# When a chunk's rows are normalised, and how the last two rows of the output are weighted, in a hybrid encoder block on one Trainium2 core

## The chip, the core and the metric

One core of a Trainium2 chip runs the whole program. Its engines work side by side, each from an instruction queue of its own: TensorE (PE, with its weight loads as PEld) multiplies matrices, VectorE (DVE), ScalarE (ACT) and GpSimd (POOL) do elementwise work, SyncE (SP) issues most of the DMA transfers; ACT issues some too. Engines wait for each other by semaphores. The metric is the device time of one execution in microseconds.

## The reference

One encoder layer over 1024 tokens of width 1024, all in float32: a combined projection, windowed attention and a bidirectional gated-DeltaNet mixer on its parts, an output projection with a residual, and a feed-forward part with squared ReLU. What matters here is the second half:

```python
def _rmsnorm(x, w):
    x32 = x.astype(jnp.float32)
    y = x32 * lax.rsqrt(jnp.mean(x32 * x32, axis=-1, keepdims=True) + EPS)
    return (y * w.astype(jnp.float32)).astype(x.dtype)
...
        h = h + jnp.concatenate([attn, gdn], axis=-1) @ w_out[l]
        hn = _rmsnorm(h, norm_ffn_w[l])
        h = h + jnp.square(jax.nn.relu(hn @ w_ffn_in[l])) @ w_ffn_out[l]
    return _rmsnorm(h, norm_final_w)
```

## The kernel before

The 1024 tokens are eight chunks of 128 rows. `h[c]` is the tile of chunk c, 128 x 1024, with tokens on the partitions. Every float32 product is made of three matmuls (`mm3`, lines 124 to 126) over a high and a low part of each operand; `split` makes the parts: ACT copies the high part (L119), POOL subtracts it (L120).

The program is written as Python generators that are woven together; a scheduler then places the instructions in one fixed queue per engine, with an eye on priorities and on free buffers of the pools. The queues are what the order listings below show.

Around the change in the middle of the program run three generators. `scan(1, ...)` goes backwards over the chunks (7 down to 0) and finishes the mixer's rows `o` of a chunk; its small products are L797. `out_all` takes the chunks in the same order. For each it prepares the mixer's part (`out_gdn`): four Squares on ACT with their sums (L900), four small steps on DVE (L902 to L905), a power on POOL (L906), a scaling on DVE (L907), four transposes on PE (L910), a multiply out of PSUM on DVE (L911), and the split. Then `out_gemm` multiplies with the output weights: two halves of twelve matmuls, each added to `h[c]` by DVE (L876). At L926 SP stores the sum to memory. Up to three chunks are prepared ahead: in the text of the program the preparation of chunk c - 3 stands right behind the sum of chunk c and ahead of the product of chunk c - 1.

The finished rows are normalised by `norm_h`, which calls `norm_rows`: a Square over the whole row on ACT with its sum (L203), two POOL steps for the reciprocal root (`rstd`, L190 and L191), and a scaling on DVE (L205). For chunks 7 to 4 the scaling writes in place, over the tile that L926 stores; for 3 to 0 it writes another tile. Before, chunks 7 to 4 are normalised together when all four are summed, at the head of `tokens_second` (`norm_half(1)`), and each of 3 to 0 when it is summed, if four rows are there already. `tokens_second` transposes the four rows on PE (L209) into feed-forward operands (L966, L214, L215, L970, L949, L950). It is woven with the rest of `out_all`.

At the end of the program `second_products` makes the last product group P4, row by row, for rows 4 to 7; each row's sum is finished by DVE (L1199), and `finish` normalises it: Square on ACT (L1229), `rstd` on POOL, one DVE instruction that scales and weights (L1232), and a store from SP (L1233). The last row, 7, is finished by `finish_last` in two halves of 512 columns, the upper of which is complete earlier; its halves are scaled by ACT (L1220) and DVE (L1221) and stored from ACT and SP (L1223).

Of the kernel before, what the change touches and what calls it, by code (L numbers as in the profile page):

```python
# [11 lines left out]
BF16 = mybir.dt.bfloat16  # L12
AF = mybir.ActivationFunctionType
ALU = mybir.AluOpType
AX = mybir.AxisListType

P = 128
SEQ = 1024
D = 1024
NT = SEQ // P  # L20
NK = D // P
HALF = 512
GH = 4
DFF = 4096
EPS = 1e-6
# [52 lines left out]
class Block:  # L78
# [837 lines left out]
    def out_all(self, chunks):  # L916
# [3 lines left out]
        for n, c in enumerate(chunks):  # L920
# [6 lines left out]
            self.summed.append(c)  # L927
            if c < 4 and len(self.rows) >= 4:
                self.norm_h(c)

# [247 lines left out]
    def second_products(self, n, p, left, right, banks, last):  # L1178

        nc = self.nc  # L1180
        bank, tag = {"P1": ("a", "psA"), "P2": ("b", "psB"), "P5": ("c", "psB"), "P7": ("d", "psA"), "P6": ("a", None),
                     "P3": ("c", None), "P4": ("d", None)}[p]
        lo, hi = slice(0, HALF), slice(HALF, D)
        for i in range(4):
            ps = banks[bank, i] = self.ps(tag) if tag else banks[bank, i]
# [10 lines left out]
            if p == "P4" and last and i == 3:  # L1196
                self.finish_last(7, ps)
                continue
# [4 lines left out]
            if last and p in ("P3", "P4"):  # L1203
                self.finish(i if p == "P3" else 4 + i)

    def finish_last(self, t, ps):

        nc = self.nc
        lo, hi = slice(0, HALF), slice(HALF, D)
        h = self.h[t]  # L1210
        ss, rs = self.small((P, 2)), self.small((P, 1))
        scr, hw, o = self.pt((P, HALF), BF16), [self.pt(), self.pt()], [self.pt(), self.pt()]
        nc.scalar.activation(out=scr, in_=h[:, hi], func=AF.Square, accum_out=ss[:, 1:2])
        nc.gpsimd.tensor_tensor(out=hw[1], in0=h[:, hi], in1=self.w_fin[:, hi], op=ALU.mult)
        nc.vector.tensor_tensor(out=h[:, lo], in0=h[:, lo], in1=ps, op=ALU.add)
        nc.scalar.activation(out=scr, in_=h[:, lo], func=AF.Square, accum_out=ss[:, 0:1])
        nc.vector.tensor_tensor(out=hw[0], in0=h[:, lo], in1=self.w_fin[:, lo], op=ALU.mult)
        nc.vector.tensor_tensor(out=ss[:, 0:1], in0=ss[:, 0:1], in1=ss[:, 1:2], op=ALU.add)
        self.rstd(ss[:, 0:1], rs)
        nc.scalar.activation(out=o[0], in_=hw[0], func=AF.Copy, scale=rs)  # L1220
        nc.vector.tensor_scalar(out=o[1], in0=hw[1], scalar1=rs, scalar2=None, op0=ALU.mult)  # L1221
        for i, sl in enumerate((lo, hi)):
            (nc.scalar, nc.sync)[i].dma_start(out=self.io["out"][0, t * P:(t + 1) * P, sl], in_=o[i])  # L1223

    def finish(self, t):
# [152 lines left out]
```

## Time and profile before

| | |
|---|---|
| runs | 1255.85, 1256.17, 1258.47 us; median 1256.17 |
| the profiled execution | 1255.02 us, of which the span of the trace is 1253.3 |
| mean granted clock of TensorE | 0.983 of full speed |
| matmuls and transposes on PE | 6482 |

A row of the timeline reads: start in us, duration in us, engine, line, operation, output tile <- inputs, shapes, count; in brackets the idle time of the engine ahead of it and what ended that. On PE the printed duration is longer than the distance to the next matmul, since matmuls are pipelined; distances are taken from the starts. Rows of stages give, for each stretch, the busy time of PE, PEld, DVE, ACT and POOL with the number of instructions, the granted clock of TensorE as a share, the DMA engines' busy share and GB/s.

### The profile page before, as it was taken

Reading aid. Unit: us, or ns where it says so; the run is one execution under the profiler, and the core shown is the slowest. Engines: PE = TensorE matmul, PEld = TensorE weight load, DVE = VectorE, ACT = ScalarE, POOL = GpSimd, SP = SyncE. Lnnn points to the kernel's source line nnn. Section 1 sums busy time; section 2 is a strip of 40 time slices with the busy share of each in tenths; the row PEclk is TensorE's granted clock in tenths of the full one; section 3 lists DMA queues with packets and bytes.
Section 4 is the critical chain, followed back from the end, with each engine's and each line's share of the span. In section 5 each row is a group of like instructions: output and inputs, shape, how many; then the busy total and the mean of one; then the engine's idle time right before and its main releaser. Section 6 shows DMA issues by size and latency. Waiting matters only on the chain.

```text
span 1253.3 us, 18527 instructions
## 1 busy us (share of the span) xinstructions
PE 1191.6 (95%) x6482; PEld 967.2 (77%) x6482; DVE 854.9 (68%) x1528; ACT 621.4 (50%) x1347; POOL 580.3 (46%) x488
## 2 busy tenths in 40 slices
PE   7999999899789989998999999999999999999997
PEld 5778777677568868877788888888777888888885
DVE  5667667982389986676655454544668797886976
ACT  6455688335485752125464554545545434444343
POOL 5354211362432433144573534535445665655595
PEclk9999999899889999998999999999999999999999
DMA  7134344441956678122234344443678624434323
GB/s 239 52 121 133 101 171 140 139 126 40 223 168 158 190 216 296 60 84 85 84 131 159 132 151 143 154 159 134 223 280 280 223 85 167 151 121 148 95 90 135
DMA packets 121630, 187.62 MB, mean 150 GB/s; under 512 B 11043, under 2 KB 64416, under 8 KB 121537
## 3 DMA queue, kind: packets, MB, share of 16 engines
q1 hardware_dynamic: 96708, 152.58, 37.9%
q10 hardware_dynamic: 16381, 29.67, 6.3%
q0 software_dynamic: 8448, 4.20, 1.9%
q8 instruction: 51, 0.84, 0.3%
q14 instruction: 42, 0.34, 0.1%
HBM read 122.39 MB, written 63.49 MB: 148 GB/s over the span
## 4 chain that ended last, share of the span: by engine, by line
PE 49%; DVE 6%; DMA 3%; issue 2%; POOL 1%; ACT 1%; ACTq 0%; POOLq 0%; DVEq 0%; SPq 0%
PE psA L124 8%; PE psA L125 8%; PE psA L126 8%; PE psB L126 7%; PE psB L125 7%; PE psB L124 7%; DMA pg<-sd 3%; PE psB L797 2%; DVE pg L1154 1%; DVE pt L1163 1%; DVE wr L1166 1%; PE psB L209 1%; DVE pg L1199 1%; DMA sd<-pt 0%; DVE wr L1161 0%
## 5 line engine op out<-in xcount | busy, mean ns | idle before, releaser
L124 PE MATMUL psA<-pg,wh 128*128 128x512 f32 x416 | 167.6, 404 | 2.1 <-ACT pt L458 2.1
L126 PE MATMUL psA<-pg,wl 128*128 128x512 f32 x416 | 166.9, 401 | 0.0
L125 PE MATMUL psA<-pg,wh 128*128 128x512 f32 x416 | 166.5, 400 | 0.0
L120 POOL TENSOR_TENSOR wl<-wr,wh 128x512 fp32r<-128x512 f32 x44 | 70.2, 1618 | 154.0 <-ACT wh L119 153.9
L1154 DVE TENSOR_TENSOR pg<-pg 128x512 fp32r<-128x512 f32 x112 | 122.7, 1127 | 18.8 <-ACT pg L1153 18.6
L120 POOL TENSOR_TENSOR wh<-wr,wh 128x512 fp32r<-128x512 f32 x32 | 47.9, 1518 | 131.5 <-ACT wh L119 131.5
L1071 ACT ACTIVATE pt<-pt 128x512 f32<-128x512 f32 x64 | 40.4, 632 | 122.7 <-DVE pt L1061 122.7
L125 PE MATMUL psA<-pg,pg 128*128 128x512 f32 x256 | 99.7, 391 | 0.5 <-POOL pg L120 0.5
L124 PE MATMUL psA<-pg,pg 128*128 128x512 f32 x256 | 99.0, 391 | 1.0 <-DVE pg L1199 1.0
L126 PE MATMUL psA<-pg,pg 128*128 128x512 f32 x256 | 99.7, 389 | 0.0
L120 POOL TENSOR_TENSOR pg<-wr,pg 128x512 fp32r<-128x512 f32 x48 | 73.4, 1560 | 51.0 <-ACT pg L119 51.0
L124 PEld LDWEIGHTS psA<-pg,wh 128*128 128x128 f32 x416 | 79.2, 190 | 21.3 <-ACT pt L458 2.4
L125 PEld LDWEIGHTS psA<-pg,wh 128*128 128x128 f32 x416 | 79.3, 191 | 19.7 <-issue 0.9
L126 PEld LDWEIGHTS psA<-pg,wl 128*128 128x128 f32 x416 | 79.1, 190 | 18.6
L1153 ACT CAST pg<-pg 128x512 fp32r<-128x512 f32 x112 | 67.2, 620 | 41.3 <-DMA pg<-sd 31.0
L126 PE MATMUL psB<-pg,pg 128*128 128x512 f32 x192 | 75.0, 390 | 1.3 <-DVE pg L1154 1.3
L125 PE MATMUL psB<-pg,pg 128*128 128x512 f32 x192 | 75.0, 391 | 0.8 <-POOL pg L120 0.7
L124 PE MATMUL psB<-pg,pg 128*128 128x512 f32 x192 | 74.7, 390 | 0.4 <-ACT pg L1153 0.4
L119 ACT CAST wh<-wr 128x512 fp32r<-128x512 f32 x76 | 43.6, 623 | 45.5 <-PE psA L125 24.8
L1061 DVE TENSOR_TENSOR pt<-psB,pt 128x512 f32<-128x512 f32 x39 | 26.9, 689 | 55.1 <-PE psB L126 30.1
L1061 DVE TENSOR_TENSOR pt<-psA,pt 128x512 f32<-128x512 f32 x39 | 26.8, 689 | 55.0 <-PE psA L126 39.5
L124 PEld LDWEIGHTS psA<-pg,pg 128*128 128x128 f32 x256 | 48.0, 188 | 12.6 <-DVE pg L1199 2.3
(385 smaller groups left out, 3307.7 us busy)
## 6 DMA issues: line engine op xcount, KB each, us to landing
sd<-pt ACTq DMA_DIRECT2D x112, 256.0 KB, 2.2
pg<-sd SPq DMA_DIRECT2D x112, 256.0 KB, 2.9
wr<-in_w_ffn_in SPq DMA_DIRECT2D x32, 512.0 KB, 3.8
wr<-in_w_in SPq DMA_DIRECT2D x22, 512.0 KB, 4.8
pg<-in_x SPq DMA_DIRECT2D x16, 512.0 KB, 5.4
wr<-in_w_ffn_out SPq DMA_DIRECT2D x16, 512.0 KB, 4.8
sc<-kvd SPq DMA_DIRECT2D x14, 512.0 KB, 4.1
kvd<-pt SPq DMA_DIRECT2D x16, 256.0 KB, 2.8
```

Of the source, the lines that this page charges most:

```text
L119: nc.scalar.copy(out=h, in_=raw)
L120: (eng or nc.gpsimd).tensor_tensor(out=l, in0=raw, in1=h.bitcast(F32), op=ALU.subtract)
L124: nc.tensor.matmul(ps, wh, xh, start=first, stop=False, skip_group_check=onto)
L125: nc.tensor.matmul(ps, wh, xl, start=False, stop=False, skip_group_check=onto)
L126: nc.tensor.matmul(ps, wl, xh, start=False, stop=last, skip_group_check=onto)
L209: self.nc.tensor.transpose(ps[:, i * P:(i + 1) * P], row[:, k * P:(k + 1) * P], self.ident)
L797: nc.tensor.matmul(ps[:, h - g.start, :], left(h), right[:, h, :], start=True, stop=True)
L1061: self.nc.vector.tensor_tensor(out=out, in0=in0, in1=in1, op=ALU.add)
L1071: self.nc.scalar.activation(out=c, in_=c, func=AF.Relu)
L1153: nc.scalar.copy(out=s[:, 0], in_=raw)
L1154: v.tensor_tensor(out=s[:, 1], in0=raw, in1=s[:, 0].bitcast(F32), op=ALU.subtract)
L1163: v.tensor_tensor(out=b["T2"], in0=b["B22"], in1=b["T1"], op=ALU.subtract)
```

## The change

Two things are changed. In `out_all`, `norm_h(c)` follows every chunk's sum, for all eight chunks; `norm_half` then finds nothing left to do. At the end, row 6 is no longer finished by `finish`: its two halves are multiplied with the weight by DVE (`weighted`, L1215 of the changed kernel), its Square and `rstd` are as before, and one DVE instruction scales it at the end of `finish_last` (L1242). In `finish_last` itself the sum of squares of the upper half is scaled by a POOL step of its own (L1230), a second POOL step joins the halves (L1234) and takes the place of a DVE addition, the multiply of the upper half on POOL is dropped, and DVE scales and weights the upper half in one instruction (L1237).

```diff
--- before.py
+++ after.py
@@ -925,8 +925,7 @@
             yield from self.out_gemm(self.h[c], *ready.pop(0), self.wo[1])
             self.nc.sync.dma_start(out=self.hd[c], in_=self.h[c])
             self.summed.append(c)
-            if c < 4 and len(self.rows) >= 4:
-                self.norm_h(c)
+            self.norm_h(c)
 
 
     def norm_h(self, c):
@@ -1194,33 +1193,54 @@
             dst = {"P1": self.h[i][:, lo], "P2": self.h[i][:, lo], "P6": u2, "P5": self.h[4 + i][:, hi],
                    "P7": self.h[4 + i][:, hi], "P3": self.h[i][:, hi], "P4": self.h[4 + i][:, lo]}[p]
             if p == "P4" and last and i == 3:
-                self.finish_last(7, ps)
+                self.finish_last(7, ps, self.held)
                 continue
             nc.vector.tensor_tensor(out=dst, in0=dst, in1=ps, op=ALU.add)
             if last and p == "P6":
                 for d in (self.h[i][:, hi], self.h[4 + i][:, hi], self.h[4 + i][:, lo]):
                     nc.gpsimd.tensor_tensor(out=d, in0=d, in1=u2, op=ALU.add)
             if last and p in ("P3", "P4"):
-                self.finish(i if p == "P3" else 4 + i)
-
-    def finish_last(self, t, ps):
+                if p == "P4" and i == 2:
+                    self.held = self.weighted(6, hw, 0)
+                else:
+                    self.finish(i if p == "P3" else 4 + i)
+                if p == "P4" and i == 1:
+                    hw = self.wr((P, D))
+                    self.weighted(6, hw, 1)
+
+    def weighted(self, t, hw, part):
+
+        nc = self.nc
+        sl = slice(part * HALF, (part + 1) * HALF)
+        nc.vector.tensor_tensor(out=hw[:, sl], in0=self.h[t][:, sl], in1=self.w_fin[:, sl], op=ALU.mult)
+        if part == 0:
+            ss, rs = self.small((P, 1)), self.small((P, 1))
+            nc.scalar.activation(out=self.pt((P, D), BF16), in_=self.h[t], func=AF.Square, accum_out=ss)
+            self.rstd(ss, rs)
+            return t, hw, rs
+
+    def finish_last(self, t, ps, held):
 
         nc = self.nc
         lo, hi = slice(0, HALF), slice(HALF, D)
         h = self.h[t]
         ss, rs = self.small((P, 2)), self.small((P, 1))
-        scr, hw, o = self.pt((P, HALF), BF16), [self.pt(), self.pt()], [self.pt(), self.pt()]
+        scr, hw, o = self.pt((P, HALF), BF16), self.pt(), [self.pt(), self.pt()]
         nc.scalar.activation(out=scr, in_=h[:, hi], func=AF.Square, accum_out=ss[:, 1:2])
-        nc.gpsimd.tensor_tensor(out=hw[1], in0=h[:, hi], in1=self.w_fin[:, hi], op=ALU.mult)
+        nc.gpsimd.tensor_scalar(out=ss[:, 1:2], in0=ss[:, 1:2], scalar1=1.0 / D, scalar2=EPS, op0=ALU.mult, op1=ALU.add)
         nc.vector.tensor_tensor(out=h[:, lo], in0=h[:, lo], in1=ps, op=ALU.add)
         nc.scalar.activation(out=scr, in_=h[:, lo], func=AF.Square, accum_out=ss[:, 0:1])
-        nc.vector.tensor_tensor(out=hw[0], in0=h[:, lo], in1=self.w_fin[:, lo], op=ALU.mult)
-        nc.vector.tensor_tensor(out=ss[:, 0:1], in0=ss[:, 0:1], in1=ss[:, 1:2], op=ALU.add)
-        self.rstd(ss[:, 0:1], rs)
-        nc.scalar.activation(out=o[0], in_=hw[0], func=AF.Copy, scale=rs)
-        nc.vector.tensor_scalar(out=o[1], in0=hw[1], scalar1=rs, scalar2=None, op0=ALU.mult)
+        nc.vector.tensor_tensor(out=hw, in0=h[:, lo], in1=self.w_fin[:, lo], op=ALU.mult)
+        nc.gpsimd.tensor_scalar(out=ss[:, 0:1], in0=ss[:, 0:1], scalar1=1.0 / D, scalar2=ss[:, 1:2], op0=ALU.mult,
+                                op1=ALU.add)
+        nc.gpsimd.tensor_tensor(out=rs, in0=ss[:, 0:1], in1=self.nhalf_exp[:, :1], op=ALU.pow)
+        nc.vector.scalar_tensor_tensor(out=o[1], in0=h[:, hi], scalar=rs, in1=self.w_fin[:, hi], op0=ALU.mult, op1=ALU.mult)
+        nc.scalar.activation(out=o[0], in_=hw, func=AF.Copy, scale=rs)
         for i, sl in enumerate((lo, hi)):
             (nc.scalar, nc.sync)[i].dma_start(out=self.io["out"][0, t * P:(t + 1) * P, sl], in_=o[i])
+        t, hw, rs = held
+        nc.vector.tensor_scalar(out=hw, in0=hw, scalar1=rs, scalar2=None, op0=ALU.mult)
+        nc.sync.dma_start(out=self.io["out"][0, t * P:(t + 1) * P, :], in_=hw)
 
     def finish(self, t):
         nc = self.nc
```

What the scheduler made of it stands in the queues. First ACT, around the preparations of chunks 4 and 3 (`pg_4322` is `o` of chunks 5 and 4, `pg_4019` of chunks 3 and 2; `pt_5653`, `pt_5679`, `pt_5705` are the split of chunks 7, 6 and 5; `wl` and `wh` rows belong to feed-forward weights). Before:

```order
L119 CAST pt_5576<-wr_5574 128x512
L900 ACTIVATE scr_5743,sm_5741<-pg_4322 128x128 x4
L900 ACTIVATE scr_5798,sm_5796<-pg_4019 128x128 x4
L119 CAST wl_5623<-wr_5612 128x512
L119 CAST wh_5617<-wr_5610 128x512
L119 CAST wh_5620<-wr_5610 128x512
L119 CAST pt_5653<-wr_5631 128x512
L900 ACTIVATE scr_5853,sm_5851<-pg_4019 128x128 x3
L119 CAST pt_5679<-wr_5657 128x512
```

In the changed kernel (`pg_4973`, `pg_5076`, `pg_5165` are `h` of chunks 7, 6 and 5):

```order
L119 CAST pt_5679<-wr_5657 128x512
L119 CAST wl_5628<-wr_5612 128x512
L119 CAST pt_5705<-wr_5683 128x512
L203 ACTIVATE pt_5740,sm_5738<-pg_4973 128x1024
L900 ACTIVATE scr_5750,sm_5748<-pg_4322 128x128 x4
L119 CAST pt_5767<-wr_5745 128x512
L203 ACTIVATE pt_5802,sm_5800<-pg_5076 128x1024
L900 ACTIVATE scr_5812,sm_5810<-pg_4019 128x128 x4
L119 CAST pt_5829<-wr_5807 128x512
L203 ACTIVATE pt_5864,sm_5862<-pg_5165 128x1024
L900 ACTIVATE scr_5874,sm_5872<-pg_4019 128x128 x4
```

The four L900 of each chunk have moved from far ahead of the splits to behind the Square (L203) of a row: those of chunk 4 behind the Square of chunk 7, those of 3 behind that of 6, those of 2 behind that of 5.

PE at the same place, the end of chunk 7's product (`psA_5723`), the transposes of chunk 4 (L910) and the product of chunk 6 (`psA_5764`, in the changed kernel `psA_5771`). Before:

```order
L126 MATMUL psA_5723<-pg_5039,pt_5654 128x512
L910 MATMUL psA_5754<-ident,wr_5739 128x128 x4
L124 MATMUL psA_5764<-pg_5224,pt_5679 128x512
L125 MATMUL psA_5764<-pg_5225,pt_5679 128x512
L126 MATMUL psA_5764<-pg_5224,pt_5680 128x512
L124 MATMUL psA_5764<-pg_4936,pt_5679 128x512
L797 MATMUL psB_5474<-sc_5320,pg_3791 128x128 x2
L125 MATMUL psA_5764<-pg_4937,pt_5679 128x512
L797 MATMUL psB_5479<-sc_5409,pt_5411 128x128 x2
L797 MATMUL psB_5502<-sc_5409,pg_3790 128x128 x2
```

After:

```order
L797 MATMUL psB_5542<-sc_5409,pg_3791 128x128 x2
L797 MATMUL psB_5516<-sc_5497,pg_2527 128x128
L797 MATMUL psB_5547<-sc_5498,pt_5500 128x128 x2
L797 MATMUL psB_5551<-sc_5409,pg_3791 128x128 x2
L797 MATMUL psB_5556<-sc_5498,pt_5500 128x128 x2
L910 MATMUL psA_5761<-ident,wr_5746 128x128 x4
L124 MATMUL psA_5771<-pg_5224,pt_5679 128x512
L125 MATMUL psA_5771<-pg_5225,pt_5679 128x512
L126 MATMUL psA_5771<-pg_5224,pt_5680 128x512
```

The transposes of chunk 4 stand directly ahead of chunk 6's product in both; the scan's products (L797), which stood among its matmuls, now all stand ahead of the transposes. Further on the same holds for L910 of chunk 3 ahead of chunk 5's product and of chunk 2 ahead of chunk 4's. Behind chunk 4's product now stand 20 of the row transposes (L209), L910 of chunk 1, the product of chunk 3, 12 row transposes, L910 of chunk 0 and the product of chunk 2; before, the products of chunks 4 and 3 followed each other, then all 32 row transposes.

DVE around the additions of chunk 6 (`pg_5076`). Before (`wr_5794` is the preparation of chunk 3, `sm_5906` that of chunk 1):

```order
L907 TENSOR_TENSOR wr_5794<-pg_4019,sm_5797 128x512
L836 SCALAR_TENSOR_TENSOR pg_3794<-psB_5474,egc,pg_3794 128x128 x2
L843 TENSOR_TENSOR pg_3794<-pg_3794,psB_5479 128x256
L810 SCALAR_TENSOR_TENSOR sc_5497<-psB_5502,negc,sc_5497 128x128 x2
L810 SCALAR_TENSOR_TENSOR sc_5497<-psB_5507,negc,sc_5497 128x128 x2
L902 TENSOR_TENSOR sm_5906<-sm_5906,sq_1234 128x4
L903 TENSOR_SCALAR sm_5906<-sm_5906 128x4
L904 RECIPROCAL sm_5906<-sm_5906 128x4
L876 TENSOR_TENSOR pg_5076<-pg_5076,psA_5764 128x512
L905 TENSOR_TENSOR sm_5906<-sm_5906,sq_1234 128x4
L876 TENSOR_TENSOR pg_5076<-pg_5076,psA_5778 128x512
```

After (`wr_5808` is the preparation of chunk 3):

```order
L876 TENSOR_TENSOR pg_5076<-pg_5076,psA_5771 128x512
L876 TENSOR_TENSOR pg_5076<-pg_5076,psA_5785 128x512
L205 TENSOR_SCALAR pg_5076<-pg_5076,sm_5801 128x1024
L902 TENSOR_TENSOR sm_5810<-sm_5810,sq_1234 128x4
L903 TENSOR_SCALAR sm_5810<-sm_5810 128x4
L904 RECIPROCAL sm_5810<-sm_5810 128x4
L905 TENSOR_TENSOR sm_5810<-sm_5810,sq_1234 128x4
L907 TENSOR_TENSOR wr_5808<-pg_4019,sm_5811 128x512
L911 SCALAR_TENSOR_TENSOR wr_5807<-psA_5823,cols,wr_5808 128x512
L876 TENSOR_TENSOR pg_5165<-pg_5165,psA_5833 128x512
```

L205 of chunk 6 and the small steps of chunk 3 (L902 to L905) now stand right behind the additions, and L907 of chunk 3 behind those; before, L902 to L905 of chunk 3 stood some 50 rows further ahead, L907 ahead of the additions, and L205 of chunk 6 behind the products of chunks 6 to 3.

The last rows of DVE, before (`pg_8759` is row 6, `pg_8760` row 7):

```order
L1199 TENSOR_TENSOR pg_8759<-pg_8759,psA_11060 128x512
L1232 SCALAR_TENSOR_TENSOR wr_11245<-pg_8758,sm_11240,wl_10666 128x1024
L1215 TENSOR_TENSOR pg_8760<-pg_8760,psA_11074 128x512
L1232 SCALAR_TENSOR_TENSOR wr_11267<-pg_8759,sm_11262,wl_10666 128x1024
L1217 TENSOR_TENSOR pt_11285<-pg_8760,wl_10666 128x512
L1218 TENSOR_TENSOR sm_11282<-sm_11282 128x1
L1221 TENSOR_SCALAR pt_11288<-pt_11286,sm_11283 128x512
```

After:

```order
L1198 TENSOR_TENSOR pg_8759<-pg_8759,psA_11060 128x512
L1252 SCALAR_TENSOR_TENSOR wr_11245<-pg_8758,sm_11240,wl_10666 128x1024
L1215 TENSOR_TENSOR wr_11248<-pg_8759,wl_10666 128x512 x2
L1231 TENSOR_TENSOR pg_8760<-pg_8760,psA_11074 128x512
L1242 TENSOR_SCALAR wr_11248<-wr_11248,sm_11265 128x1024
L1233 TENSOR_TENSOR pt_11285<-pg_8760,wl_10666 128x512
L1237 SCALAR_TENSOR_TENSOR pt_11287<-pg_8760,sm_11283,wl_10666 128x512
```

Two multiplies of row 6 now stand between the weighting of row 5 and the last addition (L1231), where the weighting of row 6 stood behind it; the scaling of row 6 (L1242) stands ahead of the multiply of row 7.

## The prediction

> **What bounds the kernel now.** I read the page first, then the busy time by stretch of the part that the change touches (530 to 615 us), then that part instruction by instruction on each engine, and the last 12 us in the same way. Of the page one line is enough:
>
> ```profile
> PE 1191.6 (95%) x6482; PEld 967.2 (77%) x6482; DVE 854.9 (68%) x1528; ACT 621.4 (50%) x1347; POOL 580.3 (46%) x488
> ```
>
> PE is busy 95% of the span, so anything that makes PE wait is paid in full, and anything that another engine does beside PE is free. Two stretches, from the table by stage:
>
> ```profile
> 570.00:580.00 10.00, 9.37 (x43) 7.31 (x41) 4.26 (x7) 4.79 (x9) 4.86 (x7) 1.00 0.39 117
> 580.00:590.00 10.00, 7.03 (x37) 6.82 (x38) 7.42 (x15) 7.81 (x19) 4.54 (x8) 0.66 0.13 52
> ```
>
> The second column is PE's busy time, the one after the five engines is the granted clock. PE is full up to 579 us, and then has a hole and a clock of 0.66. These are PE's rows at the edges of that part:
>
> ```profile
> 550.46 0.39 PE L126 MATMUL psA<-pg,pt 128*128 128x512 f32 x1
> 550.69 0.60 PE L910 MATMUL psA<-ident,wr 128*128 128x128 f32 x4
> 551.04 0.48 PE L124 MATMUL psA<-pg,pt 128*128 128x512 f32 x1
> 578.98 0.40 PE L126 MATMUL psA<-pg,pt 128*128 128x512 f32 x1
> 582.97 3.25 PE L209 MATMUL psB<-ident,pg 128*128 128x128 f32 x14 [3.59 <-DVE pg L205]
> 589.87 0.47 PE L124 MATMUL psA<-pg,pt 128*128 128x512 f32 x1
> ```
>
> The product of chunk 7 ends at 550.46 + 0.23 (0.23 us is the distance of two matmuls at full clock, as from 572.96 to 573.19 and everywhere else here). That of chunk 6 begins at 551.04; only four transposes of chunk 4 lie between, 0.09 apart. From there PE has no gap until chunk 3 ends at 579.2. Then it waits 3.6 us for the last of four scaled rows (L205), transposes 8 blocks of them, and starts chunk 2 at 589.87. So **the only idle time here that an earlier normalisation can win is 3.6 us**, plus what the slow clock behind it costs.
>
> **The change in the middle of the program.** Each engine runs its instructions in the order of the program. ACT shows it:
>
> ```profile
> 525.02 0.31 ACT L900 ACTIVATE scr<-pg 128x128 f32<-128x128 f32 x1
> 575.30 1.05 ACT L203 ACTIVATE pt<-pg 128x1024 bf16<-128x1024 f32 x1
> 580.60 1.06 ACT L203 ACTIVATE pt<-pg 128x1024 bf16<-128x1024 f32 x1 [1.03 <-DVE pg L876]
> 581.66 0.29 ACT L900 ACTIVATE scr<-pg 128x128 f32<-128x128 f32 x1
> 582.07 0.31 ACT L900 ACTIVATE scr<-pg 128x128 f32<-128x128 f32 x1
> ```
>
> The second of these is the Square of chunk 7, summed at 551.6; it ran 24 us later because other instructions stood ahead of it. Now the order lists count. In before, the L900 of chunk 4 and 3 stand far ahead (the first row is the last of chunk 3), and PE finds their result ready. In the changed kernel ACT has the Square of chunk 7 and behind it the L900 of chunk 4, then the Square of 6 and behind it the L900 of chunk 3, then 5 and 2. PE has the transposes of chunk 4 ahead of the product of chunk 6, those of 3 ahead of 5, those of 2 ahead of 4. So every product now waits for a chain that begins at the end of the product before it, though its own operands are ready. DVE's queue is tied the same way: the scaling L205 of chunk c stands ahead of the small steps L902 to L905 of the next preparation. And for chunks 7 to 4 L205 writes in place, so it must wait until the store of that row to memory has landed; in before that was long past. SP's queue itself keeps its order.
>
> The chain, link by link (the row on landing is that of the eight stores of line 926):
>
> ```profile
> 572.96 0.39 PE L126 MATMUL psA<-pg,pt 128*128 128x512 f32 x1
> 573.39 0.69 DVE L876 TENSOR_TENSOR pg<-pg,psA 128x512 f32<-128x512 f32 x1 [2.11 <-PE psA L126]
> 551.60 0.33 SPq L926 DMA_DIRECT2D hd<-pg  x1
> DMA to landing us min/median/max: 3.0/3.0/3.3
> 582.16 0.75 DVE L205 TENSOR_SCALAR pg<-pg,sm 128x1024 f32<-128x1024 f32 x1 [0.72 <-POOL sm L191]
> 585.13 0.17 DVE L902 TENSOR_TENSOR sm<-sm,sq 128x4 f32<-128x4 f32 x1 [0.75 <-ACT scr L900]
> 585.33 0.17 DVE L903 TENSOR_SCALAR sm<-sm 128x4 f32<-128x4 f32 x1
> 586.68 1.02 POOL L906 TENSOR_TENSOR sm<-sm,half_exp 128x4 f32<-128x4 f32 x1 [3.09 <-DVE sm L905]
> 588.73 0.68 DVE L907 TENSOR_TENSOR wr<-pg,sm 128x512 f32<-128x512 f32 x1
> ```
>
> From the start of a chunk's last matmul: the add begins 0.43 later and takes 0.69 (1.12); the store is issued 0.02 behind it and lands 3.0 later (4.14); L205 starts 0.05 later and frees DVE after 0.67 (4.86); four small steps at 0.20 (5.61); POOL's power 0.15 behind them, 1.02 long (6.78); L907 0.04 later, 0.69 (7.51); PE 0.05 later (7.56). ACT lies beside it: the Square starts at 1.15, the four L900 end at about 4.0 and POOL's two steps on the row (0.86 together, as at the end of the kernel below) at 3.3, both before 4.86; without the store the chain would be 0.9 shorter. PE is idle for 7.56 - 0.23 = **7.33 us**. In before the same place costs 0.
>
> What an idle PE costs beyond that, from the clock in single microseconds and the rows at such a restart:
>
> ```profile
> 541.00:542.00 1.00, 0.46 (x2) 0.46 (x3) 1.00 (x2) 0.00 (x0) 1.00 (x1) 0.50 0.63 233
> 545.00:546.00 1.00, 1.00 (x6) 0.83 (x5) 0.49 (x2) 0.34 (x1) 0.58 (x1) 1.00 0.14 41
> 582.00:583.00 1.00, 0.03 (x1) 0.04 (x1) 0.75 (x1) 0.84 (x5) 0.88 (x2) 0.50 0.70 279
> 588.00:589.00 1.00, 1.00 (x8) 1.00 (x7) 1.00 (x3) 1.00 (x3) 0.00 (x0) 0.63 0.00 0
> 541.54 1.11 PE L910 MATMUL psA<-ident,wr 128*128 128x128 f32 x4 [0.67 <-DVE wr L907]
> 542.31 0.78 PE L124 MATMUL psA<-pg,pt 128*128 128x512 f32 x1
> 543.31 0.63 PE L126 MATMUL psA<-pg,pt 128*128 128x512 f32 x1
> 543.73 0.63 PE L124 MATMUL psA<-pg,pt 128*128 128x512 f32 x1
> ```
>
> At a clock of 0.50 matmuls are 0.42 to 0.43 us apart and four transposes take 0.77. The slow stretch lasted about 3 us at the first place and 5.6 us at the second. Each microsecond of it loses 1 - 0.232/0.427 = 0.46, so a restart loses 1.4 to 2.6 us; I take the middle, 2.0. A product of 24 matmuls, 5.66 us at full clock (24 times 0.2325 and the first one's 0.08), becomes 7.66.
>
> The Trainium skill, "TensorE: Matmul & The Clock Gate", part 1, says that the clock is halved after a whole idle window of some 3.4 us and freed after a whole busy one, in windows that run freely. By that rule an idle time of 7.33 us always holds such a window, and a restart is slow for 3.4 to 6.8 us; an estimate from the page's figures is 2.3 us lost instead of 2.0, 1.2 us more in all. The two stretches of the trace, 3 and 5.6 us, agree with it.
>
> Now PE's timetable. **Chunk 6**: the store of chunk 7 is issued at 551.60 as before and lands at 554.6, L205 ends at 555.3. Between it and L905 DVE's new order has seven pieces of the scan that before ran beside PE's products; a row of four such pieces prices them:
>
> ```profile
> 553.92 1.12 DVE L810 SCALAR_TENSOR_TENSOR sc<-psB,negc,sc 128x128 f32<-128x128 f32 x4
> ```
>
> 7 times 0.28 is 2.0, the small steps 0.75 (558.1), power, L907 and hand-overs 1.95 (560.0), slow transposes 0.77: the product starts at 560.8 instead of 551.04 and ends at 568.5. All of the scan's own products are now behind it. At the least the chain here is as short as elsewhere (550.46 + 7.56 = 558.0), 2.0 less. **Chunk 5**: 568.5 + 7.33 + 0.77 = 576.6, ends 584.3. **Chunk 4**: 592.4, ends 600.1. **The row transposes** (L209) need L205 of chunk 4: last matmul at 599.9, + 4.19 + 0.75 + 0.05 = 604.9. In before this point was 582.97, with chunk 3 done as well. The order now puts 20 of the transposes here (0.20 apart at slow clock, 32 of them from 582.97 to 589.5: 4.0), four of chunk 1 (0.4), then **chunk 3** (5.66 and 0.3 for the end of the slow stretch), to 615.3, then 12 more (1.1), to 616.4. **Chunk 2** waits for the preparation of chunk 0. Its four L900 stand on ACT behind the Square of chunk 3 and three pieces of the token blocks, its small steps on DVE behind L205 and five more pieces, POOL's power behind a subtraction of the blocks (some 1.4). Adding the durations along that order gives 10.1 from the last matmul of chunk 3 at 615.1 to the transposes, 625.2, and 625.6 for the product. Before: 589.87. The shift is **35.7 us**, and the restart there loses another 2.0: 37.7. At least, with the short chain of 6.7 (no store: here L205 writes another tile), it is 3.4 less; at most, if the pieces meet POOL at the wrong moment, some 2 more.
>
> Behind chunk 2 both programs have the same order on every engine up to the last rows, and PE there is the chain, so nothing gives the shift back; the FFN only starts later. The 3.6 us hole does not vanish, it is one of the longer ones.
>
> **The change at the end.**
>
> ```profile
> 1242.65 1.28 DVE L1232 SCALAR_TENSOR_TENSOR wr<-pg,sm,wl 128x1024 f32<-128x1024 f32 x1
> 1244.77 0.69 DVE L1215 TENSOR_TENSOR pg<-pg,psA 128x512 f32<-128x512 f32 x1 [0.83 <-PE psA L126]
> 1245.37 1.84 DVE L1232 SCALAR_TENSOR_TENSOR wr<-pg,sm,wl 128x1024 f32<-128x1024 f32 x1
> 1246.08 0.19 ACT L1216 ACTIVATION_READ_ACCUMULATOR pt<-pg 128x1 f32 x1
> 1247.14 0.68 DVE L1217 TENSOR_TENSOR pt<-pg,wl 128x512 f32<-128x512 f32 x1
> 1247.97 0.19 POOL L190 TENSOR_SCALAR sm<-sm 128x1 f32<-128x1 f32 x1 [1.84 <-DVE sm L1218]
> 1248.83 0.72 ACT L1220 ACTIVATE pt<-pt,sm 128x512 f32<-128x512 f32 x1 [2.56 <-POOL sm L191]
> 1249.58 0.34 ACTq L1223 DMA_DIRECT2D out<-pt  x1
> ```
>
> Now POOL waits for DVE, which is held by the weighting of row 6 (1.84). After, POOL takes the sum of squares straight from ACT. DVE does two multiplies of row 6 (0.61 from start to start, as L1217) behind the weighting of row 5 (free at 1243.86, 0.07 before its end, as the weighting of row 6 shows), so the last add starts at 1245.08, 0.31 late. ACT's read-out ends 1.50 after the add's start, 1246.58; POOL's two steps start 0.10 later and take 0.86 as now (1247.97 to 1248.83): 1247.54 instead of 1248.83. **1.3 us earlier**, and the last store with it. The scaling of row 6 (0.75) and the last multiply (0.68) fit into the 1.77 us between; without that cover the scaling would cost its 0.7. The small POOL step on the upper half is done before it is needed. What is late next is the last store.
>
> **The sum.** 37.7 - 1.3 = 36.4. The profiled execution took 1255.02 us (span 1253.3 and 1.7 around it, taken as unchanged), which becomes 1291.4. The median of the runs is 1.15 above it: 1256.17 + 36.4 = **1292.6 us**.
>
> **Rivals.** (1) The clock does not fall in the new holes: four restarts less at 2.0, 8.0 less, 1284.6 us. Against it: it fell in a hole of 3.6 us. (2) The clock stays low through the whole part, as PE is busy only half the time: each of four products takes 24 times 0.43 = 10.3 instead of 7.66, 10.6 more, 1303.2 us. Against it: it came back within 5.6 us at half load. The skill's page named above speaks against both, since a product of 7.66 us always holds a whole busy window and the hole a whole idle one. (3) **The other side**: the change does what its words say and no more. If the next preparation is done while PE still multiplies, the four rows are scaled in time, the hole of 3.6 us goes, the 32 transposes run at 0.09 instead of 0.20 (3.5), and with the end's 1.3 the kernel is 8.4 us faster, 1247.8. It is decided by whether the L900 of chunk 3 can run ahead of the Square of chunk 6. For it: their input is ready early (525 us in before). Against it: ACT's order, and the Square that waited 24 us in the rows above. The same page of the skill says that ACT's and DVE's queues are strictly first in, first out; by that this rival falls.
>
> **Chances and range.** The forecast 0.81, the warm clock 0.07, the slow clock throughout 0.07, the faster kernel 0.05. Down from 1292.6 the bounds are 2.4 (restarts), 2.0 (chunk 6), 3.4 (chunk 2), up 2.4 (restarts), 2 (chunk 2) and 1.2 (four landings at 3.3, the longest, instead of 3.0): 1284.8 to 1298.2; a little more on each side for parts that I may have missed, and rival 1 inside: 1282 to 1300. A measurement of this kernel tells some 0.2% from no change, 2.5 us: faster 0.05, the same 0.01, slower 0.94.
>
> **What would show it.** PE idle four times for 5 to 9 us between 550 and 630 us, each time released by L907 (or L205 ahead of the row transposes); granted clock 0.5 behind each; L902 of chunks 3 and 2 directly behind an L205 that waits for a DMA; L209 first near 605 and chunk 2's product near 625 us. At the end POOL released by ACT, the last add 0.3 us late behind the two multiplies. I am wrong if PE shows no holes there, or if the part behind 630 us shrinks by as much.

## The result, and the profile after

The changed kernel takes 1292.23 us (median of 4 runs, 1288.82 to 1293.62) beside 1256.01 us for the kernel before (4 runs, 1254.44 to 1258.47): **1.0284 times as long, 95% interval 1.0261 to 1.0306**. Its profiled execution took 1292.52 us with a span of 1290.5.

The busy times on the page of the changed kernel, and three stretches from its table by stage (columns as before):

```profile
PE 1205.2 (93%) x6482; PEld 975.8 (76%) x6482; DVE 854.1 (66%) x1529; ACT 621.5 (48%) x1347; POOL 576.8 (45%) x488
```
```profile
570.00:580.00 10.00, 3.13 (x12) 2.32 (x11) 3.47 (x8) 3.26 (x11) 1.76 (x4) 0.64 0.13 52
580.00:590.00 10.00, 6.19 (x21) 4.59 (x19) 1.70 (x3) 2.65 (x10) 2.02 (x3) 0.84 0.22 79
560.00:630.00 70.00, 40.65 (x158) 33.12 (x157) 26.34 (x53) 20.90 (x57) 16.99 (x20) 0.74 0.14 47
```

PE, full up to 579 us before, now works 40.65 of the 70 us from 560 to 630, at a mean clock of 0.74. No other engine is full there either: nothing is short of work or of bandwidth, everything waits in turn. The timeline shows on what:

```profile
562.83 1.11 PE L910 MATMUL psA<-ident,wr 128*128 128x128 f32 x4 [2.70 <-DVE wr L907]
577.36 1.12 PE L910 MATMUL psA<-ident,wr 128*128 128x128 f32 x4 [6.87 <-DVE wr L907]
593.06 1.11 PE L910 MATMUL psA<-ident,wr 128*128 128x128 f32 x4 [6.87 <-DVE wr L907]
605.25 4.53 PE L209 MATMUL psB<-ident,pg 128*128 128x128 f32 x20 [4.30 <-DVE pg L205]
626.06 1.11 PE L910 MATMUL psA<-ident,wr 128*128 128x128 f32 x4 [8.61 <-DVE wr L907]
```

These are the transposes ahead of the products of chunks 6, 5 and 4, the row transposes, and those ahead of chunk 2. The chain of the second hole, on DVE, SP, ACT and POOL:

```profile
570.53 0.69 DVE L876 TENSOR_TENSOR pg<-pg,psA 128x512 f32<-128x512 f32 x1 [2.10 <-PE psA L126]
571.25 0.33 SPq L926 DMA_DIRECT2D hd<-pg  x1
571.31 1.06 ACT L203 ACTIVATE pt<-pg 128x1024 bf16<-128x1024 f32 x1 [5.93 <-DVE pg L876]
573.65 0.31 ACT L900 ACTIVATE scr<-pg 128x128 f32<-128x128 f32 x1
573.98 0.75 DVE L205 TENSOR_SCALAR pg<-pg,sm 128x1024 f32<-128x1024 f32 x1 [2.77 <-DMA hd<-pg]
574.65 0.16 DVE L902 TENSOR_TENSOR sm<-sm,sq 128x4 f32<-128x4 f32 x1
575.26 0.17 DVE L905 TENSOR_TENSOR sm<-sm,sq 128x4 f32<-128x4 f32 x1
575.57 1.01 POOL L906 TENSOR_TENSOR sm<-sm,half_exp 128x4 f32<-128x4 f32 x1 [2.19 <-DVE sm L905]
576.61 0.69 DVE L907 TENSOR_TENSOR wr<-pg,sm 128x512 f32<-128x512 f32 x1 [1.19 <-POOL sm L906]
```

And the landing of the eight stores of that line in the changed kernel, 2.6/2.6/3.5 where it was 3.0/3.0/3.3:

```profile
DMA to landing us min/median/max: 2.6/2.6/3.5
```

It is the predicted chain: sum, store, scaling, four small steps, power, scaling, and PE 0.06 later. ACT ends its four Squares at 574.06 (the read-out behind the fourth), 0.6 us before L902, so the store decides by that much only. The end, on DVE, ACT and POOL:

```profile
1281.82 1.29 DVE L1215 TENSOR_TENSOR wr<-pg,wl 128x512 f32<-128x512 f32 x2
1283.02 0.68 DVE L1231 TENSOR_TENSOR pg<-pg,psA 128x512 f32<-128x512 f32 x1
1284.34 0.19 ACT L1232 ACTIVATION_READ_ACCUMULATOR pt<-pg 128x1 f32 x1
1284.70 0.40 POOL L1234 TENSOR_SCALAR sm<-sm 128x1 f32<-128x1 f32 x1 [0.92 <-ACT pt L1232]
1285.18 0.55 POOL L1236 TENSOR_TENSOR sm<-sm,nhalf_exp 128x1 f32<-128x1 f32 x1
```

POOL is released by ACT as forecast, but starts 0.17 behind the read-out's end and takes 0.40 for a step that took 0.19 before.

### The profile page after: what moved, and what is told of

Read it like the earlier page. It is cut to its first block, busy times and chain, and to the rows that moved or that the text cites. A ratio compares the mean times of both kernels' runs of the same rounds, so it can differ in the third digit from the quotient of the medians.

```text
span 1290.5 us, 18531 instructions
## 1 busy us (share of the span) xinstructions
PE 1205.2 (93%) x6482; PEld 975.8 (76%) x6482; DVE 854.1 (66%) x1529; ACT 621.5 (48%) x1347; POOL 576.8 (45%) x488
## 3 DMA queue, kind: packets, MB, share of 16 engines
q1 hardware_dynamic: 96708, 152.58, 36.4%
## 4 chain that ended last, share of the span: by engine, by line
PE 48%; DVE 6%; issue 3%; DMA 3%; POOL 2%; ACT 1%; POOLq 0%; DVEq 0%; ACTq 0%
PE psA L124 9%; PE psA L125 9%; PE psA L126 9%; PE psB L124 7%; PE psB L125 7%; PE psB L126 7%; DMA pg<-sd 2%; PE psB L797 1%; POOL pg L120 1%; DVE pt L1162 1%; DVE wr L1165 1%; DVE pg L1198 1%; PE psA L910 0%; PE psB L209 0%; DVE wr L1160 0%
## 5 line engine op out<-in xcount | busy, mean ns | idle before, releaser
L1153 DVE TENSOR_TENSOR pg<-pg 128x512 fp32r<-128x512 f32 x112 | 123.5, 1136 | 20.3 <-ACT pg L1152 20.1
```

The source lines that it names most:

```text
L1153: v.tensor_tensor(out=s[:, 1], in0=raw, in1=s[:, 0].bitcast(F32), op=ALU.subtract)
```

## The experiments

The measured stretch in this table runs from the transposes of chunk 6 (535.75 us before, the last piece of PE that is alike in all) to the first product of the feed-forward part (624.94 before): each from two rows of the run's own trace. It leaves out what differs between executions ahead of it. The clock is the mean of the stretch from 560 to 630 us. Each ratio is taken against the kernel before as timed beside that run, where its median lay between 1255.34 and 1257.88 us, so it does not follow from the first row.

| run | median, us | against the kernel before, 95% interval | stretch, us | clock |
|---|---|---|---|---|
| kernel before | 1256.01 | | 89.19 | 0.95 |
| changed kernel | 1292.23 | 1.0284 (1.0261 to 1.0306) | 125.79 | 0.74 |
| changed, again | 1291.87 | 1.0278 (1.0252 to 1.0304) | 125.88 | 0.73 |
| end alone | 1257.94 | 1.0001 (0.9986 to 1.0017) | 90.03 | |
| normalisation alone | 1293.96 | 1.0276 (1.0253 to 1.0299) | 123.29 | 0.76 |
| normalised behind the next preparation | 1251.10 | 0.9947 (0.9931 to 0.9964) | 84.29 | 1.00 |
| normalised two preparations later | 1257.43 | 0.9994 (0.9982 to 1.0006) | 88.33 | 0.95 |
| holes filled with products | 1285.44 | 1.0218 (1.0194 to 1.0243) | 120.82 | 0.93 |
| scaled rows in another tile | 1285.67 | 1.0229 (1.0209 to 1.0249) | 118.52 | 0.78 |
| the same, again | 1286.64 | 1.0242 (1.0217 to 1.0267) | 118.75 | 0.78 |
| changed, transposes one product later | 1252.36 | 0.9975 (0.9958 to 0.9992) | 85.97 | 0.95 |
| both later | 1242.72 | 0.9902 (0.9880 to 0.9925) | 75.91 | 1.00 |
| before, transposes one product later | 1249.48 | 0.9947 (0.9927 to 0.9967) | 80.45 | 0.98 |

The stretch itself varies with the clock. In it the run with the end alone has the order of the kernel before and the same hole of 3.59 us, and is 0.84 us longer; the run with the normalisation alone has the order of the changed kernel and its holes (2.70, 6.88, 6.88, 4.30 and 8.62), and is 2.5 us shorter. What differs in both is how long the clock stays low behind a restart. Differences of less than 2.5 us in this column say little.

### The two halves of the change

The end alone keeps the old condition in `out_all`:

```diff
-            self.norm_h(c)
+            if c < 4 and len(self.rows) >= 4:
+                self.norm_h(c)
```

> Only the end of the program is changed; the chunks are normalised as before. Theory (the whole slowdown comes from the place of the earlier normalisation, the end wins a little): no new holes of PE between 550 and 630 us, the hole of 3.6 us ahead of the row transposes is still there, and the time is 0.6 us (what the changed kernel's own trace shows) to 1.3 us (the term of the prediction) below the kernel before, some 1255 us. Rival (the end costs part of the 36 us): above 1260 us.

The normalisation alone is the kernel before with

```diff
-            if c < 4 and len(self.rows) >= 4:
-                self.norm_h(c)
+            self.norm_h(c)
```

> Only the normalisation is moved; the end is that of the kernel before. Theory: the holes of the changed kernel (2.7, 6.9, 6.9, 4.3 and 8.6 us) are all there, chunk 2's product starts some 34 us later than before, and the time is 36 to 38 us above the kernel before, 1292 to 1294 us. Rival (the end costs part of it): below 1285 us.

The whole slowdown is in the normalisation: 36.1 us in the second run (1293.96 against 1257.88 measured beside it), and nothing that can be told from zero in the first. What the end wins is under the resolution of the times. The traces give it: from the start of the last sum of row 6 to the end of the span it is 11.25 us before, 10.48 in the changed kernel and 10.62 in the run with the end alone, so 0.6 to 0.8 us and not the 1.3 predicted.

### Where the row's normalisation stands

One preparation later (`norm_h` returns at once for a row that is done):

```diff
                 ready.append(self.out_gdn(chunks[n + len(ready)]))
+            if n:
+                self.norm_h(chunks[n - 1])
...
-            self.norm_h(c)
+        self.norm_h(chunks[-1])
```

> As the changed kernel, but a chunk's normalisation stands behind the next preparation, one product later. Theory (the cost is the chain between two products, through the queues of ACT and DVE): the chain of about 7.2 us from one late add to the next now lies beside one product with its transposes (6.0 us), so each hole of 6.9 us shrinks to 1.0 to 1.7 us, the clock stays above 0.9, and the time is 1250 to 1261 us. Rival (the cost is the early normalisation itself, its instructions and its traffic, wherever it stands): the holes stay near 7 us and the time near 1290 us.

The same work in another place is not slow at all: 41 us less than the changed kernel, and 0.5% faster than the kernel before. In that place early normalisation costs nothing. Two holes are left, of 1.50 and 1.57 us. The trace of this run shows their chain:

```profile
573.37 0.65 PE L910 MATMUL psA<-ident,wr 128*128 128x128 f32 x4 [1.50 <-DVE wr L907]
574.06 0.75 DVE L911 SCALAR_TENSOR_TENSOR wr<-psA,cols,wr 128x512 f32<-128x512 f32 x1 [0.75 <-PE psA L910]
574.84 0.62 ACT L119 CAST pt<-wr 128x512 fp32r<-128x512 f32 x1 [5.30 <-DVE wr L911]
575.37 1.05 ACT L203 ACTIVATE pt<-pg 128x1024 bf16<-128x1024 f32 x1
577.79 0.75 DVE L205 TENSOR_SCALAR pg<-pg,sm 128x1024 f32<-128x1024 f32 x1 [0.24 <-POOL sm L191]
578.46 0.16 DVE L902 TENSOR_TENSOR sm<-sm,sq 128x4 f32<-128x4 f32 x1
580.42 0.69 DVE L907 TENSOR_TENSOR wr<-pg,sm 128x512 f32<-128x512 f32 x1
581.17 0.66 PE L910 MATMUL psA<-ident,wr 128*128 128x128 f32 x4 [1.57 <-DVE wr L907]
```

It no longer begins at a sum. It is a loop from one preparation's transposes to the next's: multiply, split on ACT, the row's Square behind the split, the four Squares, the scaling, the small steps, the power, and the transposes, 7.80 us for a product that needs 6.0 with its transposes.

Two preparations later (`n > 1`, `chunks[n - 2]`):

> As the changed kernel, but a chunk's normalisation stands two preparations later. Theory: with a slack of two products (12 us against a chain of 7.5 us) no product waits, the old hole of 3.6 us and the slow transposes behind it (3.5 us) are won, and with 0.6 us of the end the time is 1247 to 1250 us, a hole of at most 1 us ahead of chunk 2 included. Rival (early rows win nothing, since another wait takes the place of the hole): 1254 to 1257 us. Rival (the early normalisation itself costs): near 1290 us.

A miss: no gain. Two holes of 1.56 us and one of 0.47 replace the old 3.6, so the last sum comes 2.4 us earlier, counted as in the table. Then it is lost. These are DVE's rows behind it, and PE's first feed-forward product:

```profile
604.82 0.69 DVE L876 TENSOR_TENSOR pg<-pg,psA 128x512 f32<-128x512 f32 x1 [1.45 <-PE psA L126]
609.15 1.79 DVE L205 TENSOR_SCALAR sc<-pg,sm 128x1024 f32<-128x1024 f32 x1
610.86 1.76 DVE L1049 TENSOR_TENSOR pt<-wr,pt 128x512 f32<-128x512 f32 x1
614.94 0.75 DVE L215 SCALAR_TENSOR_TENSOR pg<-psB,cols,pg 128x512 fp32r<-128x512 f32 x1 [2.32 <-ACT pg L214]
624.39 0.77 PE L124 MATMUL psB<-pg,wh 128*128 128x512 f32 x1 [0.23 <-DVE pt L1006]
```

The third and fourth of them in the kernel before (its scaling, at 610.22, is shown in the last section):

```profile
611.91 1.77 DVE L1045 TENSOR_TENSOR pt<-wr,pt 128x512 f32<-128x512 f32 x1
615.49 0.75 DVE L215 SCALAR_TENSOR_TENSOR pg<-psB,cols,pg 128x512 fp32r<-128x512 f32 x1 [1.80 <-ACT pg L214]
```

From the last sum to the first feed-forward product DVE's queue sets the pace: 18.05 us before (606.89 to 624.94), 19.57 here. The scaling and the instruction behind it take 1.8 us in both. What differs is that three more pieces of the token blocks stand on DVE ahead of the scaling, so that it starts 4.33 us behind the last sum instead of 3.33, and that DVE then waits 2.32 us for ACT instead of 1.80. That is 1.5 of the 2.4 us. The rest goes with the clock in this execution: it is 0.50 from 624 to 628, where it was 1.00 before. In the run with the normalisation one preparation later the scaling of that row takes 0.75, other pieces fill the wait, and the same way takes 17.47.

### The price of the clock

Products that nobody uses fill four of the holes; the output is the same. In `out_gemm`, behind each sum (`fill` is 22, 22, 10 and 28 for chunks 6, 5, 4 and 3, else 0):

```diff
+            for _ in range(fill * nh):
+                nc.tensor.matmul(ps, wo[3][0][:, 0:P], wo[3][0][:, 0:HALF], start=True, stop=True)
```

> As the changed kernel, with products that nobody uses on PE in four of the holes (behind the sums of chunks 6, 5, 4 and 3: 22, 22, 10 and 28 matmuls of 128 x 512); the output is the same. Theory (an idle PE lowers the clock, and each restart loses about 2 us): PE waits 0.4 to 1.3 us instead of 6.9, 6.9, 4.3 and 8.6, the clock stays above 0.9 from 570 to 632 us, and the time is 6 to 9 us below the changed kernel, 1283 to 1286 us. Rival (the clock costs nothing, the products behind the holes are bound by something else): within 1.5 us of the changed kernel, or above it by what the added products overrun.

The clock stays up (0.93 instead of 0.74), and the time is 6.8 us below the changed kernel, inside the expected 6 to 9. The two ratios differ by 0.0066, each with some 0.0023 either way, so the price is known to about 4 us. PE waits 0.81, 3.31, 0.93 and 1.64 us there, two of them longer than the 0.4 to 1.3 expected. In the hole of 3.3 us a store took twice its usual time to land; why is open:

```profile
583.11 0.33 SPq L928 DMA_DIRECT2D hd<-pg  x1
588.27 0.75 DVE L205 TENSOR_SCALAR pg<-pg,sm 128x1024 f32<-128x1024 f32 x1 [5.18 <-DMA hd<-pg]
```

### The wait for the store

```diff
-        self.rows[c] = self.norm_rows(self.h[c], self.sc((P, D)) if c < 4 else None)
+        self.rows[c] = self.norm_rows(self.h[c], self.sc((P, D)) if c < 4 else self.pg((P, D)))
```

> As the changed kernel, but the scaled rows of chunks 7 to 4 go to another tile, so that no scaling waits for a row's store to land. Theory (the chain has the store and ACT's Squares side by side, and ACT's are almost as long): each of the holes released by L907 behind chunks 6 and 5 gets 0.5 to 0.9 us shorter, 6.0 to 6.4 instead of 6.9 us, and the time is 1 to 3 us below the changed kernel, 1289 to 1291 us. Rival (the wait for the store is what makes the holes): they shrink by 2.8 us or more each, and the time is below 1284 us.

> The changed kernel once more, as the measure for the next run: 1288 to 1295 us, holes of 2.7, 6.9, 6.9, 4.3 and 8.6 us.

> The changed kernel with the scaled rows in another tile once more. The first time it was 6.6 us below the changed kernel, though its holes were only 2.2 us shorter in sum (2.2, 6.3, 6.3, 3.7, 8.6 us); its trace also has a shorter slow stretch at the first hole. Theory (the rest was the clock in single executions): 2 to 4.5 us below the changed kernel of the same call. Rival (a shorter hole changes the clock in a regular way, as the first hole of 2.2 us no longer slows it): 5.5 to 8 us below.

The holes did what the theory said, in both traces of this kernel; these are from the first:

```profile
558.53 0.66 PE L910 MATMUL psA<-ident,wr 128*128 128x128 f32 x4 [2.22 <-DVE wr L907]
571.09 1.11 PE L910 MATMUL psA<-ident,wr 128*128 128x128 f32 x4 [6.31 <-DVE wr L907]
585.24 1.11 PE L910 MATMUL psA<-ident,wr 128*128 128x128 f32 x4 [6.25 <-DVE wr L907]
596.64 4.53 PE L209 MATMUL psB<-ident,pg 128*128 128x128 f32 x20 [3.73 <-DVE pg L205]
```

They are 0.48, 0.56, 0.62 and 0.57 shorter, 2.2 us together. The time fell by 6.6 and, in the second pair, by 5.2 us, so my expectation of 1 to 3 was wrong and the repeated one fell between its two theories. The trace accounts for it: up to the first of these rows the other tile is 3.2 us ahead of the changed kernel (21.74 against 24.90 from chunk 6's transposes, and 21.75 against 24.92 in the repeats), of which 0.48 is the hole. The rest is a slow clock that both traces of the changed kernel show around 542 to 547 us and neither of the other tile's. Behind that row it gains 4.1 us, 1.75 of holes and the rest clock. Two executions of each of these kernels agree, but two other runs with the changed kernel's order up to that row took 23.44 us (normalisation alone) and 23.76 (holes filled) where it took 24.90, with a shorter slow stretch at 543 to 546. So up to 1.5 of the 3.2 us can be chance of the executions traced. Why the clock falls at 542 in one kernel and not in the other, ahead of all that differs between them, stays open.

### Where the transposes stand

`out_gdn` is cut in two. The four transposes with the multiply and the split move to `out_turn`, which is called one product later:

```diff
-            while len(ready) < 3 and n + len(ready) < len(chunks) and chunks[n + len(ready)] in self.scanned:
-                ready.append(self.out_gdn(chunks[n + len(ready)]))
+            while n + len(ready) + len(rows) < min(n + 3, len(chunks)) and chunks[n + len(ready) + len(rows)] in self.scanned:
+                if rows:
+                    ready.append(self.out_turn(*rows.pop(0)))
+                rows.append(self.out_gdn(chunks[n + len(ready) + len(rows)]))
+            while rows and len(ready) < 2:
+                ready.append(self.out_turn(*rows.pop(0)))
```

> As the changed kernel, each chunk normalised right behind its sum, but the four transposes of a preparation with what follows them stand one product later in the program. Theory (the 36 us are the price of a transpose that stands in PE's queue ahead of a product that is ready): the chain of 7.3 to 7.6 us now lies beside a product of 5.6 us, so the holes ahead of the transposes shrink from 6.9 to 1.0 to 2.0 us, the hole of 4.3 us ahead of the row transposes stays, and the time is 1256 to 1265 us. Rival (the chain itself, on ACT and DVE, sets the pace wherever the transposes stand): above 1280 us.

With the normalisation left right behind each sum, this alone takes 39.5 us off the changed kernel. The time is even 3.6 us below the expected range. Of the holes ahead of the transposes 1.31 and 3.56 us are left (1.0 to 2.0 had been expected), and the row transposes do not wait at all, where I had expected 4.3: they too stand one product later now, and their scaling is done meanwhile.

```profile
570.24 0.66 PE L914 MATMUL psA<-ident,wr 128*128 128x128 f32 x4 [1.31 <-DVE wr L907]
589.81 1.11 PE L914 MATMUL psA<-ident,wr 128*128 128x128 f32 x4 [3.56 <-DVE wr L907]
```

> Both steps: the normalisation stands behind the next preparation, and the transposes one product later. Theory (the loop from one chunk's transposes over the split, the row's Square, the four Squares and the small steps to the next chunk's transposes, 7.8 us in the run with the normalisation behind the next preparation, is cut): no hole above 0.5 us ahead of the transposes or the row transposes, and the last sum 2 to 3 us earlier than there. The time is 1246 to 1250 us. Rival (what is won there is lost on DVE behind the last sum, as with the normalisation two preparations later): 1250 to 1256 us.

1242.72 us, **1.0% faster than the kernel before** and 3 us better than expected. The last sum comes 8.7 us earlier than in the run with the normalisation one preparation later (58.17 us behind chunk 6's transposes instead of 66.82), where I had expected 2 to 3. PE's rows of the same places, no wait ahead of these transposes, and the first feed-forward product:

```profile
560.40 0.60 PE L914 MATMUL psA<-ident,wr 128*128 128x128 f32 x4
569.08 0.60 PE L914 MATMUL psA<-ident,wr 128*128 128x128 f32 x4
575.10 0.60 PE L914 MATMUL psA<-ident,wr 128*128 128x128 f32 x4
581.11 0.71 PE L209 MATMUL psB<-ident,pg 128*128 128x128 f32 x5
581.65 0.60 PE L914 MATMUL psA<-ident,wr 128*128 128x128 f32 x4
612.84 0.47 PE L124 MATMUL psB<-pg,wh 128*128 128x512 f32 x1 [0.69 <-DVE pt L1013]
```

> The kernel before with nothing changed but the transposes of a preparation one product later; the chunks are normalised where they were, and so is the end. It tells what of the 12.6 us that the run with both steps later won over the kernel before comes from the earlier normalisation. Theory (both are needed: without the earlier normalisation the hole of 3.6 us ahead of the row transposes and the slow clock behind it stay, and DVE's idle time behind the last sum too): 1249 to 1254 us, with a hole of 3 to 4 us ahead of the row transposes. Rival (the later transposes alone won it): 1242 to 1246 us.

Of the 12.6 us about 6.0 come without the earlier normalisation; the other 6.6 are what it wins once nothing waits for it (the end's 0.6 to 0.8 among them). By the intervals in the table this 6.6 is known to about 4 us; the stretches differ by 4.5. My expectation of a hole of 3 to 4 us ahead of the row transposes was wrong here: they start at 583.06 without a wait.

Part of what the later transposes win lies ahead of the earlier normalisation's place. In the kernel before, the transposes of chunk 5 (541.54) stand ahead of chunk 7's product; PE waits 1.51, 0.37 and 0.67 us between 537 and 542, and the mean clock from 540 to 544 is 0.62. With the transposes one product later, chunk 7's product runs first: PE works 15.7 to 15.9 of the 16 us from 536 to 552, where it worked 13.45, and the clock stays at 1.00. This is so in all three runs of this section.

## Why the prediction was right

**The mechanism.** The three claims on order held: four Squares behind a row's Square on ACT, small steps behind a scaling on DVE, transposes ahead of a ready product on PE. PE's order is what turns the chain into idle time: with the transposes one product later the kernel wins back 39.5 us, more than the 36.2 it had lost, since it also closes the waits at 537 to 542 that the kernel before has. ACT's and DVE's order makes the chain: with the row's steps one preparation later it wins back 41. Either is enough, so the loss belongs to the two together.

**The timetable.** By the store of chunk 7 the changed execution is 3.3 us late (issued at 554.88 instead of 551.60). 2.2 of it are there at 495 us already, ahead of all that the change touches; the rest is a longer slow stretch at 542 to 549. Without these 3.3 the steps compare so, each from the rows shown above:

| step | predicted, us | measured |
|---|---|---|
| transposes ahead of chunk 6 start | 560.0 | 559.55 |
| to those ahead of chunk 5 | 15.8 | 14.53 |
| to those ahead of chunk 4 | 15.8 | 15.70 |
| to the row transposes | 13.3 | 12.19 |
| to the transposes ahead of chunk 2 | 20.3 | 20.81 |

The shift at chunk 2's product is 33.7 us instead of 35.7. The chain was taken 0.46 too long (6.87 instead of 7.33): 0.3 is the store, which landed 2.6 us after its issue and not 3.0, the rest the small steps. The restarts were slow for 3.2 to 5.7 us, where 3 to 5.6 had been read from the trace of before (the prediction calls these in agreement with 3.4 to 6.8 us, but the 3 lies below that, as the 3.2 does); behind the first hole and the third it was the shorter time, which explains the short steps. The restart at chunk 2's product cost 1.8 us (18.83 from its start to the last sum, 17.02 before), where 2.0 had been set; of that 1.0 came back in the 640 us behind it, which is within what single executions differ there.

Of the signs named, "PE idle four times for 5 to 9 us" held for three holes (6.87, 6.87 and 8.61). Ahead of chunk 6's product PE waits only 2.70 us, as the scan's products fill the rest of the chain, and ahead of the row transposes 4.30.

**The end** is the term that was mis-sized: 0.6 to 0.8 us in place of 1.3. The last add is 0.28 late (0.31 predicted). From the end of ACT's read-out to the end of POOL's second step it is 1.20 us (1284.53 to 1285.73), where 0.96 had been set: the first step takes 0.40 instead of 0.19 and starts 0.17 behind the read-out instead of 0.10. And from the issue of the last store to the end of the span it is 3.95 us instead of 3.72.

**The sum.** The errors cancel in part: 3.3 from before chunk 7, 33.7, 0.85, less 0.6, is 37.2 in the span where 36.4 were predicted. The medians differ by 36.2, which is nearer, since the offset of 2.2 us belongs to the one execution: in the repeated run of the changed kernel chunk 6's transposes start at 535.91, 0.16 behind the kernel before. So the time was hit to 0.4 us by terms that are each good to about 2; that it came so near is luck.

**The rivals.** The warm clock: it fell in each hole, and filling them shows what it would have been worth, 6.8 us in place of 8.0. The slow clock throughout: it came back behind each restart, at the latest after 5.7 us. The other side (the earlier rows win 8.4 us if the preparation is done in time) was rightly ruled out for this order, and its price was sound: with the preparation ahead of the row's Square the kernel is 6.8 us faster than before. The point named as deciding, whether the four Squares of chunk 3 run ahead of the Square of chunk 6, did decide.

## What to carry to other kernels

In a queue that is worked off in order, an instruction placed ahead of a ready one is a wait for everything behind it: before work is moved earlier, list for each engine what will stand behind it, and whose input that is. An operand that is needed two products later should not be finished ahead of the next product unless its chain is shorter than the work already queued; moving its last step on the bound engine one product back was worth more here than shortening the chain. And a gain counts from the next place where the engines meet: of 2.4 us won at the last sum 1.5 were lost on DVE before the feed-forward part began.

## What the runs showed of the hardware

The clock falls without one long pause. In the run with the normalisation two preparations later, from its table by stage:

```profile
619.00:620.00 1.00, 0.63 (x4) 0.42 (x4) 1.00 (x2) 0.98 (x2) 0.31 (x2) 1.00 1.03 356
620.00:621.00 1.00, 0.00 (x0) 0.00 (x0) 1.00 (x3) 0.27 (x2) 0.98 (x1) 1.00 0.21 71
621.00:622.00 1.00, 0.63 (x4) 0.42 (x4) 1.00 (x2) 1.00 (x3) 0.35 (x1) 1.00 0.00 0
622.00:623.00 1.00, 0.00 (x0) 0.00 (x0) 1.00 (x3) 0.71 (x3) 1.00 (x2) 0.62 0.00 0
```

From 619 to 623 PE works 1.26 of 4 us in short pieces, its longest pause 1.35 us, and the clock is halved within the last of them. The kernel before has nearly the same pauses (1.32 us of work from 621 to 625, 1.34 the longest) and kept 1.00. The Trainium skill, "TensorE: Matmul & The Clock Gate", part 1, speaks of at least one idle window of about 3.4 us, in windows that run freely; the free windows fit that one of two like stretches is hit, the whole idle window does not fit. Nor does it in the changed kernel's second hole: PE's last matmul ends at 570.5 and the clock is down from about 572.8.

DVE and POOL slow each other. In the kernel before, behind the last sum:

```profile
610.22 1.77 DVE L205 TENSOR_SCALAR sc<-pg,sm 128x1024 f32<-128x1024 f32 x1 [0.72 <-POOL sm L191]
610.15 2.99 POOL L120 TENSOR_TENSOR wh<-wr,wh 128x512 fp32r<-128x512 f32 x2
```

The scaling takes 0.75 where POOL does nothing beside it (573.98 in the changed kernel, above), so a full microsecond is waiting. The Trainium skill's page "SBUF — State Buffer", in its section on the two separate sides, says that GpSimd and, in some of its operations, VectorE use one port pair, which one of them holds for a whole instruction while the other blocks; the rows agree. In the run with both steps later the scaling starts first, at 599.70, and takes 0.75; POOL's subtraction, from 600.04, then takes 1.55 where 1.29 is what it takes alone.
